# Three weight buffers of 48 KB filled by 6 MB transfers, and 128 rows of one expert's weights on the lower 64 partitions, in a mixture-of-experts layer on one core

## The chip, the cores and the metric

The kernel runs on one core of a Trainium2 chip. The metric is device time in microseconds, the median of three runs. The kernel before takes 968.97 us (968.91 to 969.14). About 0.2% of that, 1.9 us, is what a measurement of this kernel can tell from no change.

On the core, TensorE (PE) multiplies matrices and transposes, VectorE (DVE) and ScalarE (ACT) work on elements and copy results out of PSUM, and SyncE (SP) issues the transfers (DMAs) from the chip's memory (HBM) into the on-chip memory (SBUF). Sixteen DMA engines carry them out.

## The reference

One layer over 272 tokens (16 learned meta tokens and a sequence of 256) of width 1024, all float32:

```
h = layer_norm(alpha * h + pool_mixer(h))      # causal pooling over windows 2, 4, 8, 16
h = layer_norm(alpha * h + moe(h))             # output drops the 16 meta tokens
moe: logits = h @ router_w + router_b; 4 of 32 experts per token, softmax over the 4
     each expert e:  (clamped_swiglu(x @ w1[e] + b1[e]) @ w2[e] + b2[e]) * gate
```

`w1[e]` is 1024 x 2048 (8 MB) and `w2[e]` 1024 x 1024 (4 MB). All 32 experts are used, so 384 MB of weights are read once.

## The kernel before, in words

A prologue (L151 to L338) mixes, normalises and routes the tokens. Each expert has 64 places (`CAP`) for tokens; a branch for more tokens than that stands at the end of the program and is not taken here.

Then a loop over the 32 experts, two to a pair. Of each expert:

- `load_w1` (L345) fetches `w1[e]` as two transfers of 4 MB into two buffers of a ring, each holding four blocks of 128 rows (32 KB on each of 128 partitions). `load_w2` (L355) fetches `w2` as one transfer of 4 MB into a third buffer. The ring has four buffers (`W_BUFS`). A load is issued on SP's queue when the buffer it takes has been read for the last time; SP issues in the order of the program.
- `mlp_in` (L388) is 8 steps over the blocks k of `w1`, four matmuls each: the expert's 64 gathered tokens are the stationary operand and the weights stream past. Steps 0 to 3 need the first transfer, 4 to 7 the second.
- `swiglu` (L399): ACT copies the two halves out of PSUM (`hs`, L403), PE transposes them back (L406), DVE and ACT apply bias, clamp and gate.
- `finish(e - 1)` runs `mlp_out` (L436) of the expert before: 16 matmuls with `w2[e - 1]` as the streaming operand, and two copies into `y`.
- For an odd expert, `combine` (L458) adds the pair before to `acc` by matmuls with `srow` (L462), and `prepare` (L539) gathers the next pair's tokens (`gather`, L131, matmuls at L138).

From expert 28 on the sums are kept in PSUM: `onto` (L561, L566) takes the place of `combine`. Expert 29 is finished in its own iteration (L613 to L617), so its `w2` is loaded right after its `w1`. The last transfers are `w1[31]` (8 MB, in pieces), `w2[30]` (4 MB) and `w2[31]` in two column halves (`load_w2_halves`, 4 MB, in pieces); behind them `mlp_out_half` (L447, L451) does expert 31 by halves, then come the last sums, the layer norm (`store`, L492) and four output transfers.

The order on each engine is the program's, except where `tc.issue_after` moves a block behind a named instruction. In the printed order a matmul on float32 counts once, in the profile twice.

Of the kernel before, what the change touches and what calls it, by code (L numbers as in the profile page):

```python
# [17 lines left out]
P = 128  # L18
# [15 lines left out]
W_BUFS = 4  # L34
# [7 lines left out]
def moe_trunk(ctx: ExitStack, tc: tile.TileContext, x, pool_w, aux_in, b1_in, w1, w2, w2_last, b2, out):  # L42
# [46 lines left out]
    b2r = const.tile([E + 1, D], F32, name="b2r")  # L89
# [62 lines left out]
    b1_b = const.tile([P, D], F32, name="b1_b")  # L152
    xg0 = columns()
    d0 = mid.tile([P, NT, 2, CAP], F32, tag="disp", name="d0")
    with tc.tile_pool(name="pro", bufs=1) as pro:
# [5 lines left out]
        pw = pro.tile([P, G, 2, GD], F32, name="pw")  # L161
# [45 lines left out]
        uT = pro.tile([P, G, 2, SEQ], F32, name="uT")  # L207
# [137 lines left out]
    def load_w1(src, pieces=((0, 4), (0, 4))):  # L345
        v = src.rearrange("(i p j) f -> i p j f", p=P, j=4)
        ts = []
        for i, js in enumerate(pieces):
            wt = wpool.tile([P, 4, 2 * D], F32, tag="w", name="w1t")
            for j, j2 in zip(js, js[1:]):  # L350
                nc.sync.dma_start(out=wt[:, j:j2], in_=v[i][:, j:j2])
            ts.append(wt)
        return lambda k: ts[k // 4][:, k % 4, :]

    def load_w2(src, js=(0, KC)):  # L355
        v = src.rearrange("(p j) f -> p j f", j=KC)
        wt = wpool.tile([P, KC, D], F32, tag="w", name="w2t")
        for j, j2 in zip(js, js[1:]):
            nc.sync.dma_start(out=wt[:, j:j2], in_=v[:, j:j2])
        return lambda k: wt[:, k, :].rearrange("p (c o s) -> p o c s", c=2, o=2)  # L360

    def load_w2_halves():

        ts = wpool.tile([P, 2, KC, 512], F32, tag="w", name="w2h")
# [23 lines left out]
    def mlp_in(xcols, w1k):  # L388
        ph = [bank_h() for _ in range(2)]
        for k in range(KC):  # L390
            wk = w1k(k)
            for u in range(2):
                for hf in range(2):
                    last[k // 4] = nc.tensor.matmul(ph[u][hf * CAP:(hf + 1) * CAP], lhsT=xcols(k),  # L394
                                                    rhs=wk[:, u * D + hf * 512:u * D + (hf + 1) * 512],
                                                    start=(k == 0), stop=(k == KC - 1))
        return ph

    def swiglu(ph, bias, banks=(bank_t, bank_t)):  # L399
        pre = []  # L400
        for u in range(2):
            hs = work.tile([P, 512], F32, tag="hs", name="hs", bufs=3)
            nc.scalar.copy(hs, ph[u])  # L403
            pt = banks[u]()
            for j in range(4):
                nc.tensor.transpose(pt[:, j * P:(j + 1) * P], hs[:, j * P:(j + 1) * P], ident)  # L406
            a = work.tile([P, KC, CAP], F32, tag=f"a{u}", name=f"a{u}", bufs=1)
            nc.vector.tensor_add(a, pt.rearrange("p (c s) -> p c s", s=CAP),  # L408
                                 bias[:, :, u].unsqueeze(2).to_broadcast([P, KC, CAP]))
# [45 lines left out]
    def outputs():  # L455
        return work.tile([P, 2, 512], F32, tag="y", name="y", bufs=2)
# [13 lines left out]
    def add_rest():  # L470

        for i in range(2):
            sl = slice(i * 512, (i + 1) * 512)
            p = spread(g0T, i, bank_o())
            for t in range(NT):
                r = work.tile([P, 512], F32, tag="hs", name="rest", bufs=3)
                nc.vector.tensor_mul(r, h[:, t, sl], p)
                nc.vector.scalar_tensor_tensor(acc[:, t, sl], r, DN_ALPHA, acc[:, t, sl], op0=ALU.mult, op1=ALU.add)
# [3 lines left out]
        gT = work.tile([E + 1, SEQ], F32, name="gT")  # L482
# [29 lines left out]
    def overflow():  # L512

        with tc.For_i(0, E, 1) as e:
# [8 lines left out]
            w1k = load_w1(w1[ds(e, 1)].rearrange("e d f -> (e d) f"))  # L523
            w2k = load_w2(w2[ds(e, 1)].rearrange("e d f -> (e d) f"))
# [12 lines left out]
    pairs, acts, w2s, last = {}, {}, {}, [None, None]  # L537

    def prepare(pair, to=bank_t, banks=(bank_o, bank_o)):  # L539
        d = dispatched(place[:, :, 2 * pair:2 * pair + 2])  # L540
        s = slot_rows(d, gates[:, :, 2 * pair:2 * pair + 2], to)
        xg = columns()
        gather(d, xg, banks)
        pairs[pair] = s, outputs(), xg

    def finish(e, to=bank_y):
        pair, i = divmod(e, 2)
        mlp_out(acts[e], w2s[e], pairs[pair][1], i, to)

    pairs[0] = None, None, xg0  # L550
# [19 lines left out]
    for e in range(E):  # L570
        pair, i = divmod(e, 2)
        w1k = load_w1(w1[e], ((0, 4), (0, 4)) if e < E - 1 else ((0, 2, 4), (0, 2, 3, 4)))

        for x in range(max(e - 1, 0), e + (e == E - 3)):
            if e <= E - 3:
                w2s[x] = load_w2(w2[x])
        if i == 0:
            xg = pairs[pair][-1]
        ph = mlp_in(lambda k: xg[k // 4][:, k % 4, i * CAP:(i + 1) * CAP], w1k)
        if e == 0:  # L580
            with tc.issue_after(last[1].ins):
                pairs[0] = slot_rows(d0, gates[:, :, 0:2]), outputs(), xg0
        elif e < E - 3 and i and pair:
            s, y, _ = pairs[pair - 1]
            with tc.issue_after(last[0].ins):
                combine(y, s, pair == 1)
        elif e == E - 3:
            s, y, _ = pairs[pair - 1]
            with tc.issue_after(last[0].ins):
                onto(y, s, slice(0, 512))  # L590
# [112 lines left out]
```

## Time and profile before

| | |
|---|---|
| median of three runs | 968.97 us |
| the profiled execution, own time | 969.74 us |
| its span, first to last instruction | 968.0 us |
| PE busy | 890.0 us (92% of the span) |
| DVE, ACT busy | 237.9, 133.0 us |
| mean granted TensorE clock | 0.976 of full speed |
| moved from and to HBM | 407 MB, 420 GB/s over the span |

The span leaves 1.74 us of the execution's own time outside it. A row of the timeline or of the chain of waits gives the start in us from the start of the span, the duration, the engine, the line of the kernel and what is written and read (`ps_h<-w1t,xg`: the PSUM tile `ps_h` from `w1t` and `xg`). In square brackets stands how long the engine was idle before and who ended that. A window's row gives the busy time of each engine in a stretch, then the granted TensorE clock (PEclk), the mean busy share of the 16 DMA engines and the GB/s that they moved. L394 is `mlp_in`, L443 `mlp_out`, L451 `mlp_out_half`, L406 the transposes of `swiglu`, L462 and L566 the sums over a pair, L138 the gather.

### The profile page before, as it was taken

What the parts mean: (1) busy time and instruction counts of PE and PEld (TensorE: products, weight loads), DVE (VectorE), ACT (ScalarE), POOL (GpSimd) and SP (SyncE); (2) the same over time, 40 slices, a digit from 0 to 9 for tenths busy, and PEclk for the clock granted to TensorE, in tenths of its full rate; (3) what the DMA queues carried; (4) which work ended last, traced back from release to release, by engine and by line L of the source; (5) the groups of instructions that cost most, each with busy time, mean ns of one, the idle gap of its engine ahead of it and who ended that gap; (6) DMA issues with size and microseconds to landing.
All of it is one profiled execution on the core that took longest, in us unless ns stands there. A gap on an engine that the chain in (4) does not pass through costs nothing.

```text
span 968.0 us, 9685 instructions
## 1 busy us (share of the span) xinstructions
PE 890.0 (92%) x4229; PEld 374.4 (39%) x4229; DVE 237.9 (25%) x495; ACT 133.0 (14%) x271; POOL 1.1 (0%) x9
## 2 busy tenths in 40 slices
PE   9999899979899899998989989899898989999994
PEld 7443433424334343343433334343343433334332
DVE  7331122212152131121311223122121311212024
ACT  1320100201002010020201102010020100102011
POOL 0000000000000000000000000000000000000000
PEclk9999999999999999999999999999899999999998
DMA  9999999999999999999999999999999999999992
GB/s 384 429 427 430 431 430 431 431 433 428 431 429 430 429 433 430 432 431 430 430 431 429 430 433 431 429 431 429 430 430 431 432 432 433 433 429 426 423 416 108
DMA packets 16937, 407.09 MB, mean 421 GB/s; under 512 B 1883, under 2 KB 2011, under 8 KB 3580
## 3 DMA queue, kind: packets, MB, share of 16 engines
q1 hardware_dynamic: 16848, 406.30, 98.0%
q8 instruction: 35, 0.57, 0.2%
q10 hardware_dynamic: 44, 0.14, 0.0%
q14 instruction: 10, 0.08, 0.0%
HBM read 405.38 MB, written 1.05 MB: 420 GB/s over the span
## 4 chain that ended last, share of the span: by engine, by line
PE 53%; DMA 45%; DVE 1%; issue 0%; ACT 0%; SPq 0%; DVEq 0%; ACTq 0%
DMA w1t<-in_w 40%; PE ps_h L394 24%; PE ps_y L443 11%; PE ps_o L138 5%; PE ps_o L462 5%; DMA w2t<-in_w 3%; DMA w2h<-in_w_last 2%; PE ps_t L406 2%; PE ps_t L180 1%; PE ps_t L443 1%; PE ps_o L566 0%; PE ps_y L103 0%; PE ps_o L489 0%; PE ps_h L227 0%; PE ps_h L138 0%; PE ps_y L451 0%
## 5 line engine op out<-in xcount | busy, mean ns | idle before, releaser
L394 PE MATMUL ps_h<-w1t,xg 128*64 128x512 f32 x2048 | 471.3, 614 | 46.6 <-DMA w1t<-in_w 46.6
L394 PEld LDWEIGHTS ps_h<-w1t,xg 128*64 128x64 f32 x2048 | 157.6, 141 | 343.6 <-issue 334.4
L443 PE MATMUL ps_y<-w2t,act 128*64 128x512 f32 x928 | 205.5, 595 | 10.2 <-DMA w2t<-in_w 9.4
L408 DVE TENSOR_TENSOR a<-ps_t,b 128x512 f32<-128x512 f32 x60 | 41.5, 692 | 401.7 <-PE ps_t L406 398.6
L443 PEld LDWEIGHTS ps_y<-w2t,act 128*64 128x64 f32 x928 | 67.5, 137 | 128.7 <-issue 113.6
L403 ACT COPY hs<-ps_h 128x512 f32<-128x512 f32 x64 | 37.5, 586 | 350.6 <-PE ps_h L394 350.4
L468 DVE TENSOR_TENSOR acc<-acc,ps_o 128x512 f32<-128x512 f32 x48 | 33.0, 688 | 137.0 <-PE ps_o L462 137.0
L138 PE MATMUL ps_o<-disp,h 128*128 128x128 f32 x448 | 59.1, 275 | 0.0
L138 PEld LDWEIGHTS ps_o<-disp,h 128*128 128x128 f32 x448 | 55.4, 192 | 7.0 <-issue 7.0
L434 DVE COPY y<-ps_y 64x512 f32<-64x512 f32 (+1 forms) x30 | 20.4, 680 | 121.8 <-PE ps_y L443 120.9
L462 PE MATMUL ps_o<-y,srow 128*128 128x512 f32 x104 | 48.1, 605 | 0.0
L143 ACT ACTIVATE xg<-ps_o,aux 128x128 f32<-128x128 f32 x56 | 21.2, 456 | 178.1 <-PE ps_o L138 178.1
L432 ACT COPY y<-ps_y 64x512 f32<-64x512 f32 x29 | 16.8, 580 | 202.6 <-DVE y L434 202.6
L406 PE MATMUL ps_t<-ident,hs 128*128 128x128 f32 x240 | 39.3, 286 | 1.9 <-ACT hs L403 0.3
L406 PEld LDWEIGHTS ps_t<-ident,hs 128*128 128x128 f32 x240 | 25.2, 141 | 32.0 <-ACT hs L403 30.1
L462 PEld LDWEIGHTS ps_o<-y,srow 128*128 128x128 f32 x104 | 18.7, 189 | 29.2 <-issue 29.2
L416 DVE TENSOR_TENSOR a<-a,sig 128x512 f32<-128x512 f32 x32 | 22.1, 692 | 10.7 <-ACT sig L414 10.7
L414 ACT ACTIVATE sig<-a 128x512 f32<-128x512 f32 x32 | 20.1, 630 | 29.8 <-DVE a L412 27.3
L146 DVE TENSOR_SCALAR xg<-ps_o,aux 128x128 f32<-128x128 f32 x60 | 22.8, 405 | 2.8 <-PE ps_o L138 2.7
L418 DVE SCALAR_TENSOR_TENSOR act<-a,a 128x512 f32<-128x512 f32 x32 | 22.0, 687 | 0.6
L415 DVE TENSOR_SCALAR a<-a 128x512 f32<-128x512 f32 x32 | 13.5, 421 | 0.0
L412 DVE TENSOR_SCALAR a<-a 128x512 f32<-128x512 f32 x32 | 13.4, 418 | 0.1
(165 smaller groups left out, 260.0 us busy)
## 6 DMA issues: line engine op xcount, KB each, us to landing
w1t<-in_w SPq DMA_DIRECT2D x62, 4096.0 KB, 30.0
w2t<-in_w SPq DMA_DIRECT2D x30, 4096.0 KB, 29.3
w1t<-in_w SPq DMA_DIRECT2D x3, 2048.0 KB, 27.2
w2t<-in_w SPq DMA_DIRECT2D x4, 1024.0 KB, 25.4
w2h<-in_w_last SPq DMA_DIRECT2D x3, 1024.0 KB, 21.0
w1t<-in_w SPq DMA_DIRECT2D x2, 1024.0 KB, 30.4
xT<-in_x SPq DMA_DIRECT2D x2, 544.0 KB, 5.7
pw<-in_pool_w SPq DMA_DIRECT2D x2, 512.0 KB, 7.0
```

The lines of the kernel that those rows point to most:

```text
L138: nc.tensor.matmul(p[:, (k % n) * P:(k % n + 1) * P], lhsT=h[:, t, k * P:(k + 1) * P], rhs=d[:, t].rearrange("p i s -> p (i s)"), start=(t ...
L143: gx = nc.scalar.activation(xg[0][:, k, :], pk, AF.Identity, scale=g0T[:, k:k + 1], bias=b0T[:, k:k + 1])
L146: nc.vector.tensor_scalar(xg[1][:, k - 4, :], pk, g0T[:, k:k + 1], b0T[:, k:k + 1], op0=ALU.mult, op1=ALU.add)
L394: last[k // 4] = nc.tensor.matmul(ph[u][hf * CAP:(hf + 1) * CAP], lhsT=xcols(k), rhs=wk[:, u * D + hf * 512:u * D + (hf + 1) * 512], start ...
L403: nc.scalar.copy(hs, ph[u])
L406: nc.tensor.transpose(pt[:, j * P:(j + 1) * P], hs[:, j * P:(j + 1) * P], ident)
L408: nc.vector.tensor_add(a, pt.rearrange("p (c s) -> p c s", s=CAP), bias[:, :, u].unsqueeze(2).to_broadcast([P, KC, CAP]))
L416: nc.vector.tensor_mul(gate, gate, sig)
L418: nc.vector.scalar_tensor_tensor(act.rearrange("p c s -> p (c s)"), up.rearrange("p c s -> p (c s)"), 1.0, gate.rearrange("p c s -> p (c s ...
L443: nc.tensor.matmul(py[o], lhsT=act[:, 2 * j + hf, :], rhs=wk[:, o], start=(n == 0), stop=(n == KC - 1))
L462: nc.tensor.matmul(p, lhsT=s[:, o, t * P:(t + 1) * P], rhs=y[:, o, :], start=True, stop=True)
L468: nc.vector.tensor_add(a, a, pv)
```

## The change

- The ring has three buffers of 48 KB on each partition in place of four of 32 KB (144 KB for 128 KB).
- The weights lie in HBM in two tensors with rows of 48 KB. `wp[e]` holds `w2[e - 2]` and blocks 0 and 1 of `w1[e]`; `wq[e]` holds blocks 2 to 7 of `w1[e]`. From expert 2 on an expert is two transfers of 6 MB, `wp[e]` and `wq[e]`.
- `finish(e - 2)` runs ahead of `mlp_in(e)`, where `finish(e - 1)` ran behind it. Expert 29 is finished in iteration 31, and the sum of its pair moves there too.
- Expert 0 takes `wq[0]` first and its blocks in the order 2 to 7, 0, 1. Blocks 0 and 1 of experts 0 and 1 share a buffer. Block 1 of expert 1 (128 rows, 1 MB) lies as two halves of 64 rows side by side on partitions 0 to 63, and comes in eight transfers of eight partitions each (r, r + 8, ... r + 56, 16 KB on each); its step of `mlp_in` is two steps with 64 rows each.
- To make room: `pw` and `uT` of the prologue lie in the ring's first buffer (`early`), `b2r` in `b1_b`, `gT` in an `hs` buffer, `sig` in `act`, the last `y` in `acc`; `hs` has two buffers for three and `y` one for two.

```diff
-W_BUFS = 4
+W_BUFS = 3
...
+    def ring(name):
+        return wpool.tile([P, 6 * 2 * D], F32, tag="w", name=name)
...
+        early = ring("early")
+        pw = early[:, :G * 2 * GD].rearrange("p (g c d) -> p g c d", g=G, c=2)
...
+    def w1_of(t, t2, at=W2):
+        def w1k(k):
+            f = at + 2 * D * k if k < 2 else 2 * D * (k - 2)
+            return (t if k < 2 else t2)[:, f:f + 2 * D]
+        return w1k
...
+    def load_q(src, ks=(0, 6)):
+        return load(ring("wq"), src, [2 * D * k for k in ks])
...
+        t, t2 = load(ring("w2t"), wp[E], [D * k for k in (0, 2, 4, 6, 8)]), ring("w2h")
+        ts = [v.rearrange("p (k d) -> p k d", d=512) for v in (t[:, W2:], t2[:, :KC * 512])]
...
-            hs = work.tile([P, 512], F32, tag="hs", name="hs", bufs=3)
+            hs = work.tile([P, 512], F32, tag="hs", name="hs", bufs=2)
...
-        return work.tile([P, 2, 512], F32, tag="y", name="y", bufs=2)
+        return work.tile([P, 2, 512], F32, tag="y", name="y", bufs=1)
...
-        w1k = load_w1(w1[e], ((0, 4), (0, 4)) if e < E - 1 else ((0, 2, 4), (0, 2, 3, 4)))
-
-        for x in range(max(e - 1, 0), e + (e == E - 3)):
-            if e <= E - 3:
-                w2s[x] = load_w2(w2[x])
+        if e < 2:
+            wt2 = load_q(wq[e])
+            if e == 0:
+
+
+                wt = ring("wp")
+                nc.sync.dma_start(out=wt[:, :4 * D], in_=wp[0, :, W2:])
+                nc.sync.dma_start(out=wt[:, 4 * D:6 * D], in_=wp[1, :, W2:W2 + 2 * D])
+                for r in range(8):
+                    nc.sync.dma_start(out=wt[r:CAP:8, 6 * D:10 * D], in_=w1_low[r:CAP:8])
+            w1k = w1_of(wt, wt2, 4 * D * e)
+        else:
+
+            wt = load(ring("wp"), wp[e], (0, 6 * 2 * D))
+            w1k = w1_of(wt, load_q(wq[e], (0, 6) if e < E - 1 else (0, 2, 4, 5, 6)))
+            finish(e - 2, w2_of(wt))
...
+            xl = small.tile([CAP, CAP], F32, name="xl", bufs=1)
+            nc.scalar.copy(xl, xg[0][CAP:, 1, CAP:])
+            low = [(x, wt[:CAP, f:f + 2 * D]) for x, f in ((xg[0][:CAP, 1, CAP:], 6 * D), (xl, 8 * D))]
+        ph = mlp_in(lambda k: xg[k // 4][:, k % 4, i * CAP:(i + 1) * CAP], w1k,
+                    range(KC) if e else (2, 3, 4, 5, 6, 7, 0, 1), low)
...
-        if 0 < e < E - 4:
-            finish(e - 1)
...
-        if E - 4 <= e < E - 2:
-            finish(e - 1)
...
-            finish(e, t0)
-            s, y, _ = pairs[pair]
-            onto(y, s, slice(0, 512))
```

PE in the middle of the loop, a pair's first expert and the start of its second. Before: `mlp_in` (`w1t`) of one expert, its transposes, `mlp_out` (`w2t`) of the expert before, the next `mlp_in` with the sum of the last pair (L462) in its middle:

```order
L394 MATMUL ps_h<-w1t,xg_3224 64x512 x16
L394 MATMUL ps_h<-w1t,xg_3225 64x512 x16
L406 MATMUL ps_t_3314<-ident,hs 128x128 x4
L406 MATMUL ps_t_3323<-ident,hs 128x128 x4
L443 MATMUL ps_y<-w2t,act 64x512 x16
L394 MATMUL ps_h<-w1t,xg_3224 64x512 x16
L462 MATMUL ps_o_3377<-y,srow 128x512
```

After: `mlp_out` (L453, now from `wp`) ahead of each `mlp_in` (L405: 8 from `wp`, 24 from `wq`), and the sum (L472) behind it:

```order
L453 MATMUL ps_y<-wp,act 64x512 x16
L405 MATMUL ps_h<-wp,xg_3139 64x512 x8
L405 MATMUL ps_h<-wq,xg_3139 64x512 x8
L405 MATMUL ps_h<-wq,xg_3140 64x512 x16
L417 MATMUL ps_t_3227<-ident,hs 128x128 x4
L417 MATMUL ps_t_3236<-ident,hs 128x128 x4
L453 MATMUL ps_y<-wp,act 64x512 x16
L405 MATMUL ps_h<-wp,xg_3139 64x512 x8
L405 MATMUL ps_h<-wq,xg_3139 64x512 x8
L405 MATMUL ps_h<-wq,xg_3140 64x512 x16
L472 MATMUL ps_o_3306<-y,srow 128x512
```

`mlp_out` has moved from behind an expert's transposes to ahead of its `mlp_in`, and waits with it for the same transfer.

PE at the end. Before, from `mlp_out` of expert 29 (`ps_t_3697`) and the sum of its pair (L566) on, then experts 30 and 31:

```order
L443 MATMUL ps_t_3697<-w2t,act 64x512 x16
L566 MATMUL ps_o_3514<-y,srow 128x512
L394 MATMUL ps_h<-w1t,xg_3668 64x512 x16
L394 MATMUL ps_h<-w1t,xg_3669 64x512 x16
L406 MATMUL ps_t_3760<-ident,hs 128x128 x4
L394 MATMUL ps_h<-w1t,xg_3668 64x512
L406 MATMUL ps_y<-ident,hs 128x128 x4
L394 MATMUL ps_h<-w1t,xg_3668 64x512 x15
L394 MATMUL ps_h<-w1t,xg_3669 64x512 x16
L406 MATMUL ps_t_3826<-ident,hs 128x128 x4
L443 MATMUL ps_h<-w2t,act 64x512 x16
L451 MATMUL ps_h<-w2h,act 64x256 x8
```

After, from the end of `mlp_in` of expert 30 on: its transposes, `mlp_out` of expert 29, `mlp_in` of expert 31, the sum of pair 14 (L580), then as before:

```order
L405 MATMUL ps_h<-wq,xg_3570 64x512 x16
L417 MATMUL ps_t_3657<-ident,hs 128x128 x4
L417 MATMUL ps_y<-ident,hs 128x128 x4
L453 MATMUL ps_y<-wp,act 64x512 x16
L405 MATMUL ps_h<-wp,xg_3569 64x512 x8
L405 MATMUL ps_h<-wq,xg_3569 64x512 x8
L405 MATMUL ps_h<-wq,xg_3570 64x512 x16
L580 MATMUL ps_o_3440<-y,srow 128x512
L417 MATMUL ps_t_3745<-ident,hs 128x128 x4
L453 MATMUL ps_h<-w2t,act 64x512 x16
L461 MATMUL ps_h<-w2t,act 64x256 x8
```

`mlp_out` of expert 29 and its pair's sum (the first of its four rows is shown in both) stood ahead of `mlp_in` of expert 30 and now stand on either side of `mlp_in` of expert 31.

SP's last loads. Before:

```order
L351 DMA w1t<-in_w 128x8192 x2
L351 DMA w1t<-in_w 128x4096 x3
L351 DMA w1t<-in_w 128x2048 x2
L359 DMA w2t<-in_w 128x2048 x4
L367 DMA w2h<-in_w_last 128x2048 x3
L367 DMA w2h<-in_w_last 128x1024
L367 DMA w2h<-in_w_last 128x512 x2
```

After:

```order
L366 DMA wp<-in_wp 128x12288
L366 DMA wq<-in_wq 128x4096 x2
L366 DMA wq<-in_wq 128x2048 x2
L366 DMA w2t<-in_wp 128x2048 x4
L378 DMA w2t<-in_w_last 128x2048 x2
L378 DMA w2h<-in_w_last 128x2048
L378 DMA w2h<-in_w_last 128x1024
L378 DMA w2h<-in_w_last 128x512 x2
```

Behind the last full transfer stood 16 MB in pieces (`w1[31]`, `w2[30]`, `w2[31]`); behind `wp[31]` stand 14 MB.

## Rows read from the trace of the kernel before

**Rows 1.** The page's parts on DMA queues (packets, MB, share of 16 engines), on the chain that ended last, and its first row on DMA issues (count, KB each, median us from issue to landing).

```profile
q1 hardware_dynamic: 16848, 406.30, 98.0%
q8 instruction: 35, 0.57, 0.2%
...
PE 53%; DMA 45%; DVE 1%; issue 0%; ACT 0%; SPq 0%; DVEq 0%; ACTq 0%
...
w1t<-in_w SPq DMA_DIRECT2D x62, 4096.0 KB, 30.0
```

**Rows 2.** Windows of 58.35 us (a pair of experts) in the loop: the stretch, PE, PEld, DVE, ACT and POOL busy, PEclk, DMA share, GB/s.

```profile
129.48:187.83 58.35, 53.64 (x252) 21.87 (x250) 12.93 (x26) 7.37 (x15) 0.00 (x0) 0.97 1.00 430
304.53:362.88 58.35, 54.31 (x256) 22.24 (x254) 13.28 (x27) 7.38 (x15) 0.00 (x0) 0.97 1.00 430
537.93:596.28 58.35, 53.72 (x252) 22.32 (x250) 12.95 (x26) 7.37 (x15) 0.00 (x0) 0.97 1.00 431
```

**Rows 3.** The same view at the end: while the 1 MB pieces land (rows of 8 KB on each partition), and the last 12 us of the transfers.

```profile
926.00:941.00 15.00, 14.86 (x72) 5.32 (x68) 3.43 (x6) 3.38 (x5) 0.00 (x0) 1.00 1.01 420
941.00:944.00 3.00, 2.33 (x10) 0.48 (x8) 0.45 (x1) 0.00 (x0) 0.00 (x0) 1.00 0.98 399
944.00:947.00 3.00, 2.84 (x20) 1.75 (x22) 0.24 (x1) 0.58 (x1) 0.00 (x0) 1.00 0.65 266
947.00:950.00 3.00, 2.91 (x22) 1.25 (x18) 0.05 (x1) 0.00 (x0) 0.00 (x0) 1.00 0.48 180
950.00:953.00 3.00, 2.82 (x24) 1.95 (x24) 0.58 (x2) 0.37 (x1) 0.00 (x0) 1.00 0.09 33
```

**Rows 4.** PE's timeline near the end, from the wait for the second half of `w1[30]` (expert 30, blocks 4 to 7) on.

```profile
911.57 7.09 PE L394 MATMUL ps_h<-w1t,xg 128*64 128x512 f32 x32 [0.78 <-DMA w1t<-in_w]
918.59 0.66 PE L406 MATMUL ps_t<-ident,hs 128*128 128x128 f32 x4
...
941.57 1.94 PE L443 MATMUL ps_h<-w2t,act 128*64 128x512 f32 x8 [0.17 <-DMA w2t<-in_w]
944.16 1.95 PE L451 MATMUL ps_h<-w2h,act 128*64 128x256 f32 x16 [0.66 <-DMA w2h<-in_w_last]
...
950.18 0.40 PE L451 MATMUL ps_y<-w2h,act 128*64 128x256 f32 x1 [0.28 <-DMA w2h<-in_w_last]
```

**Rows 5.** The chain of waits at the end (start, us, what): the last transfer in it, the last matmul on a weight, what follows it.

```profile
929.08 20.97 DMA w2h<-in_w_last
...
955.07 0.06 PE ps_t L451
955.12 0.02 issue
955.14 0.38 ACT y L432
```

**Rows 6.** The chain of waits in the loop: `mlp_out`, the sum of a pair, half an `mlp_in`, a group of transposes.

```profile
535.56 7.04 PE ps_y L443 x32
...
569.49 8.78 PE ps_h L394 x32
578.27 3.63 PE ps_o L462 x8
...
584.14 7.02 PE ps_h L394 x32
591.15 0.59 PE ps_t L406 x4
```

**Rows 7.** PE's longest waits in the loop (us in total, times, longest).

```profile
PE ps_h L394 <- DMA w1t<-in_w: 46.6, 25, 3.1
PEld ps_t L406 <- ACT hs L403: 30.1, 44, 0.8
```

**Rows 8.** SP's timeline at the start: the first four loads, then the first that waited for a buffer; and PE's first `mlp_in` and the last matmul of the prologue's mixing.

```profile
3.78 3.34 SPq L351 DMA_DIRECT2D w1t<-in_w  x4
39.26 0.33 SPq L359 DMA_DIRECT2D w2t<-in_w  x1
47.14 11.73 SPq L351 DMA_DIRECT2D w1t<-in_w  x2
...
16.26 1.89 PE L227 MATMUL ps_o<-uT,pw 128*128 128x256 f32 x8
32.13 7.09 PE L394 MATMUL ps_h<-w1t,xg 128*64 128x512 f32 x32
```

More of the change, by code (lines that the diff above doesn't have):

```diff
@@ L342, in moe_trunk, with w2_of, load, load_last @@
     acc = work.tile([P, NT, D], F32, name="acc")
[L345 to L364, printed above, removed]
+    W2 = KC * D
+    def w2_of(t):
+        v = t[:, :W2].rearrange("p (n c o s) -> p n o c s", n=KC, c=2, o=2)
+        return lambda k: v[:, k]
+    def w1_of(t, t2, at=W2):
[3 more added lines that the diff above has]
+        return w1k
+    def load(t, src, cuts):
+        for f, f2 in zip(cuts, cuts[1:]):
+            nc.sync.dma_start(out=t[:, f:f2], in_=src[:, f:f2])
+        return t
+    def load_q(src, ks=(0, 6)):
+        return load(ring("wq"), src, [2 * D * k for k in ks])
+    def load_last():
+        t, t2 = load(ring("w2t"), wp[E], [D * k for k in (0, 2, 4, 6, 8)]), ring("w2h")
+        ts = [v.rearrange("p (k d) -> p k d", d=512) for v in (t[:, W2:], t2[:, :KC * 512])]
         for c, pieces in enumerate(((0, 4, 8), (0, 4, 6, 7, 8))):
             for k, k2 in zip(pieces, pieces[1:]):
-                nc.sync.dma_start(out=ts[:, c, k:k2], in_=w2_last[c, :, k:k2])
-        return [ts[:, c] for c in range(2)]
+                nc.sync.dma_start(out=ts[c][:, k:k2], in_=w2_last[c, :, k:k2])
+        return w2_of(t), ts
     def dispatched(places):
@@ L386, in slot_rows, with mlp_in @@
         return s
-    def mlp_in(xcols, w1k):
+    def mlp_in(xcols, w1k, ks=range(KC), low=None):
         ph = [bank_h() for _ in range(2)]
[L390 to L396, printed above, removed]
+        for n, k in enumerate(ks):
+            for x, wk in low if low and k == 1 else [(xcols(k), w1k(k))]:
+                for u in range(2):
+                    for hf in range(2):
+                        last[n // 4] = nc.tensor.matmul(ph[u][hf * CAP:(hf + 1) * CAP], lhsT=x,
+                                                        rhs=wk[:, u * D + hf * 512:u * D + (hf + 1) * 512],
+                                                        start=(n == 0), stop=(n == KC - 1))
         return ph
@@ L543, in prepare, with finish @@
         gather(d, xg, banks)
-        pairs[pair] = s, outputs(), xg
-    def finish(e, to=bank_y):
+        pairs[pair] = s, xg
+    def finish(e, w2k, to=bank_y):
         pair, i = divmod(e, 2)
-        mlp_out(acts[e], w2s[e], pairs[pair][1], i, to)
-    pairs[0] = None, None, xg0
+        if i == 0:
+            ys[pair] = outputs()
+        mlp_out(acts[e], w2k, ys[pair], i, to)
+    pairs[0] = None, xg0
     z = []
@@ L571, in moe_trunk @@
         pair, i = divmod(e, 2)
[L572 to L579 removed]
+        if e < 2:
+            wt2 = load_q(wq[e])
+            if e == 0:
+                wt = ring("wp")
+                nc.sync.dma_start(out=wt[:, :4 * D], in_=wp[0, :, W2:])
[7 more added lines that the diff above has]
+            finish(e - 2, w2_of(wt))
+        if i == 0:
+            xg = pairs[pair][1]
+        low = None
+        if e == 1:
+            xl = small.tile([CAP, CAP], F32, name="xl", bufs=1)
[3 more added lines that the diff above has]
+                    range(KC) if e else (2, 3, 4, 5, 6, 7, 0, 1), low)
         if e == 0:
             with tc.issue_after(last[1].ins):
[L582 to L584 removed]
+                pairs[0] = slot_rows(d0, gates[:, :, 0:2]), xg0
+        elif i and pair:
+            s = pairs[pair - 1][0]
             with tc.issue_after(last[0].ins):
[L586 to L589, printed above, removed]
[L590 removed]
+                if e < E - 3:
+                    combine(ys[pair - 1], s, pair == 1)
+                else:
+                    onto(ys[pair - 1], s, slice(0, 512))
         if e == E - 4:
```

46 lines of the change are left out of this document (25 added, 21 removed).

## The prediction

> **What bounds the kernel now.** I read the shares of the DMA queues first. The one queue that carries the data keeps the 16 engines busy for 98.0% of the span, and the chain that ended last is 45% DMA [rows 1]. In the windows of a pair the DMA share is 1.00 and the rate 430 GB/s, pair after pair, while PE works 53.6 to 54.3 of 58.35 us [rows 2]. So in the loop the transfers set the pace, and PE has 4 to 4.7 us of room per pair. PE's waits say the same: 46.6 us in all for `w1t`, never over 3.1 at once [rows 7]. That the loads keep up without a hole is read from their 30.0 us from issue to landing [rows 1]: a 4 MB transfer moves in 9.75 us (4.19 MB at 430 GB/s), so some two others lie queued ahead of each.
>
> The end is another stage. From 911.57, where PE gets the second half of `w1[30]`, to its last matmul on a weight at 955.13, PE waits for a transfer only 0.17, 0.66 and 0.28 us [rows 4, 5]. What counts there is both when the last large load lands and how much PE has left to do from then on. After 955.13 come 12.87 us (to 968.0) that the change does not touch.
>
> **The change part by part.**
>
> *Buffers, in the loop: nothing.* The bytes stay the same. With three buffers of 6 MB, `wq[e + 1]` takes the buffer of `wp[e]`. That is free when PE has done `mlp_out` (7.04) and two of the eight steps (a quarter of 2 x 7.02, 3.5) [rows 6], 10.6 us after `wp[e]` landed. SP reaches the load then. The engines need it when `wp[e + 1]` is done, two transfers of 14.6 us (6.29 MB at 430) after the landing, at 29.2. PE is late by up to some 6 us in an odd expert (`mlp_in` 10.5 behind `wq`, sum 3.63, transposes and gather 5, against 14.6), so 12 us of cover are left. If a buffer came late, SP's later loads would queue behind it and every microsecond would be lost. PE's own sum per pair stays that of [rows 2], inside 58.35. `mlp_out` no longer covers the copy to `hs` in every place; that wait is 0.8 us at a time (30.1 in 44) [rows 7], inside the 4 us of room. The waits for 6 MB instead of 4 MB can be longer (some 4 us), and behind one wait of 2.64 us half an `mlp_in` took 8.78 instead of 7.02 us [rows 6]; two of those per pair still fit into the room.
>
> *Start: nothing.* Before, four loads of 4 MB could go out ahead of PE's first `mlp_in` at 32.13, and the fifth waited until 39.26 [rows 8]. Now it is 6, 2, 1, 1 and 6 MB, 16 MB again. `wq[1]` waits for `early`, free when the mixing ends at about 18.2 [rows 8]; the 10 MB ahead of it last until 34. `wp[2]` waits for `wq[0]`, six steps behind 32.1, at 42.7; the 16 MB last until about 48. The half-row step of expert 1 costs PE four more matmuls, 1.8 us, once, in front of a wait for a load. `xl`, the shared tiles and the smaller rings (`hs`, `y`, `sig`) add no work to PE; their copies lie beside it.
>
> *Rows of 48 KB: -2.4 us.* The engines move 430 GB/s with rows of 32 KB [rows 2] and 420 with rows of 8 KB [rows 3]. Per engine that is 1219 ns for 32 KB as one row and 1248 as four, so 9.7 ns for each row more. Per 96 KB the change has two rows for three. 62 transfers of 6 MB are 24.4 MB per engine, 248 times 96 KB: 2.4 us less at the end of the loop. Rows of 48 KB do not occur before. The bounds: windows in the loop scatter by 1 GB/s, slices of the page by some 0.5% with no cause shown, so 2.4 -/+ 2.7 us. I take 2.4, the value that the two nearest row lengths give.
>
> *The eight-partition transfers: -1.2 us.* The engines do not end together: the share falls from 0.98 over 0.65 and 0.48 to 0.09 within 9 us [rows 3]. Summed from 941 (3 us times 0.98, 0.65, 0.48, 0.09), the mean engine is done at 947.6, the last about 952. If eight partitions go to eight engines, the 1 MB takes 2.4 us more on those and 2.4 less on the others (1.05 MB is 2.44 us on sixteen engines). Where the late engines are among the others, the last one can gain 2.4; where they are among the eight, it loses 2.4. No row says which. Instruction loads are 35 of 16 KB [rows 1] and are the only uneven load that I see. I take half of the gain, since an engine of the early half, now 2.4 us later, can become the last.
>
> [...]
>
> *The end: PE has more left.* Behind the second half of `w1[30]` 16 MB were still to come; behind `wp[31]` it is 14 MB. With the same bytes in all, `wp[31]` is there 2 MB later than 911.57: plus 4.9 (2.10 MB at 430), 916.45. With -2.4 and -1.2 it is 912.85. `mlp_out` of expert 29 needs it whole. PE is free just before: `wq[30]` is there 14.6 us earlier, three quarters of `mlp_in` take 10.5, the transposes some 2.3. From there PE does in a row:
>
> - `mlp_out` of 29: 7.04; `mlp_in` of 31: 14.04; the sum of pair 14: 3.63; two groups of transposes: 1.3 [rows 6];
> - `mlp_out` of 30: 7.0; then what stood between 944.16 and 955.13 less its wait of 0.28 and small gaps: 10.6 [rows 4, 5].
>
> That is 43.6 us, 10.7 of which (`mlp_out` of 29 and the pair's sum) PE used to do before 903. The transfers need only 34.0 us for the 14 MB, so from here PE sets the end: 912.85 + 43.6 = 956.45.
>
> *The sum.* 956.45 against 955.13 is +1.3 us: a span of 969.3, an execution of 971.05 (1.74 outside the span), against 969.74 of the profiled one. The median of the runs is 0.77 below that one, so I predict 970.3 us, +0.14%. A change under 0.2% can't be told from none. With the two unseen terms at their ends (rows -5.1 to +0.3, engines -2.4 to 0) `wp[31]` is there between 909 and 916.8 and the median lies between 966.4 and 974.2; the likely part of that is 968 to 972.5.
>
> **The rivals.**
>
> *The end follows the transfers, not PE (faster).* For it: the last stretch of the chain is 20.97 us of `w2h` [rows 5]. If PE makes up the 10.7 us, or if the sum above counts what overlaps, the kernel ends 3.6 us (2.4 + 1.2) earlier: 965.4. Against it: PE's sum is of rows that stand one after the other, and 43.6 is 9.6 more than 34.0.
>
> *The eight-partition transfers hit the wrong engines, or are slow (slower).* The 128 KB on each of eight engines must go somewhere. If the late engines are among the eight, `wp[31]` is there at 916.45 - 2.4 + 2.4, and the median is 973.9. It decides as soon as the eight engines lose more than about 5 us against the others, half the spread seen in [rows 3]. The same is reached if the transfers run at half speed (4.9 us more on those eight): about 974.5.
>
> [...]
>
> *Neither term exists.* Long rows gain nothing and the late engines stay late: `wp[31]` at 916.45, 973.9 us.
>
> *The queue runs dry in the loop.* If a buffer is late by 1 us once a pair, 15 us are lost: 985. Against it stand the 12 us of cover.
>
> **How the numbers follow.** The forecast has 0.50 (0.04 of it faster, 0.33 same, 0.13 slower), the end that follows the transfers 0.18, the wrong or slow engines 0.20 (0.03 same), neither term 0.07, a dry queue 0.05. That makes faster 0.22, same 0.36, slower 0.42. The range 966.2 to 975.0 holds the forecast, the wrong engines and most of the faster case's neighbourhood, and leaves out the dry queue and the lower half of the faster case.
>
> **What would show it.** Right: a DMA share of 1.00 in the windows of the loop, at 431 to 432 GB/s; PE waiting about 4 us for `wq` in odd experts; the wait for `wp[31]` ending near 913; no wait on a transfer from there on; the last weight matmul near 956.5; DMA share ending in a steeper fall. Wrong: PE waiting for `w2h` pieces at the end (the first rival); the fall of the share as long as before or longer, with `wp[31]` after 916 (the second and third); windows with a share under 0.98 in the loop (the dry queue).

## The result and the profile after

The changed kernel takes 979.61 us (median of six runs, 977.92 to 981.43) against 969.12 for the kernel before: ratio 1.0108, 95% interval 1.0097 to 1.012. It is 1.1% slower, 9.3 us above the forecast of 970.3 and outside the range of 966.2 to 975.0. The profiled execution took 979.66 us with a span of 977.8.

The page of the changed kernel: GB/s in 40 slices of 24.4 us, and the data queue [rows 1] with its share of the engines.

```profile
GB/s 380 309 443 424 443 423 439 426 435 429 425 441 419 445 422 443 423 439 425 433 431 435 429 431 435 425 440 423 439 427 433 431 435 433 431 431 433 413 382 49
...
q1 hardware_dynamic: 12656, 406.30, 97.1%
```

The second slice stands out: 309 GB/s where the loop has some 431. The windows of that place show when (columns as in [rows 2]):

```profile
26.00:31.00 5.00, 3.98 (x34) 3.35 (x33) 1.99 (x11) 3.49 (x8) 0.00 (x0) 1.00 0.97 406
32.00:37.00 5.00, 5.00 (x30) 2.31 (x30) 2.91 (x12) 0.98 (x5) 0.00 (x0) 1.00 0.57 123
```

From 32 to 37 us the engines are busy for 0.57 of the time but move only 123 GB/s. SP's timeline says what is on the queue then: `wq[0]`, two pieces of `wp` (L592, L593), the eight transfers of eight partitions (L595), and the next 6 MB, `wq[1]`, only at 36.51. Behind it stand the last three of the eight by themselves, and in a fence of their own SP's waits there (us in total, times, longest).

```profile
3.80 0.73 SPq L366 DMA_DIRECT2D wq<-in_wq  x1
4.57 0.56 SPq L592 DMA_DIRECT2D wp<-in_wp  x1
5.17 0.59 SPq L593 DMA_DIRECT2D wp<-in_wp  x1
5.80 30.58 SPq L595 DMA_DIRECT2D wp<-in_w_low  x8
36.51 0.36 SPq L366 DMA_DIRECT2D wq<-in_wq  x1
...
26.40 0.56 SPq L595 DMA_DIRECT2D wp<-in_w_low  x1
31.32 0.56 SPq L595 DMA_DIRECT2D wp<-in_w_low  x1
35.82 0.56 SPq L595 DMA_DIRECT2D wp<-in_w_low  x1
```

```profile
SPq L595 <- DMA wq<-in_wq: 15.3, 1, 15.3
SPq L595 <- DMA wp<-in_wp: 8.3, 2, 4.3
```

The sixth of the eight waits for `wq[0]` (15.3 us), the seventh and eighth for the two pieces of `wp` (8.3 us in two): each of the three waits for the load eight places before it on the queue. `wq[1]` stands behind them all, though its buffer is free from 18 us on (the third run below issues it at 18.02), and when it is issued, the eight engines that have no part in these transfers have had nothing to do for some 5 us (16 packets are under way at 31 us, 9 at 33 and 8 from 35.5 to 37.5).

The single packets of the trace, which its views don't list, add the rest: the 64 packets of 16 KB that the eight transfers consist of take a median of 1.273 us, where the 128 packets of the same size just before (L592) take 0.611. Summed up over the data queue, with a packet under way counted by its share, they give the MB moved by a time:

```
MB moved by            30 us   40 us   50 us   60 us   900 us
kernel before          11.29   15.59   19.87   24.18   385.21
changed kernel         11.35   13.20   16.94   21.27   383.37
```

2.93 MB are missing at 50 us, 6.8 us at 432 GB/s. In the loop the changed kernel is faster: from 60 to 900 us it makes good 1.07 MB, 2.5 us. The same window of both, kernel before first:

```profile
100.00:900.00 800.00, 742.28 (x3478) 305.49 (x3474) 181.05 (x347) 102.20 (x209) 0.00 (x0) 0.98 1.00 430
```

```profile
100.00:900.00 800.00, 737.63 (x3471) 301.88 (x3472) 182.90 (x353) 101.72 (x211) 0.00 (x0) 0.97 1.00 432
```

The end, where [rows 4] and [rows 5] stood for the kernel before: PE gets `wp[31]` at 920.80 and works from there to its last matmul on a weight, which starts at 964.93 and ends at 964.99, without a wait for a transfer (PE's timeline, and one row of the chain of waits).

```profile
920.80 8.69 PE L453 MATMUL ps_y<-wp,act 128*64 128x512 f32 x32 [2.65 <-DMA wp<-in_wp]
929.31 3.61 PE L405 MATMUL ps_h<-wp,xg 128*64 128x512 f32 x16
932.75 10.48 PE L405 MATMUL ps_h<-wq,xg 128*64 128x512 f32 x48
943.16 2.84 PE L580 MATMUL ps_o<-y,srow 128*128 128x512 f32 x6
945.84 1.02 PE L580 MATMUL ps_t<-y,srow 128*128 128x512 f32 x2
947.66 7.09 PE L453 MATMUL ps_h<-w2t,act 128*64 128x512 f32 x32
954.58 1.90 PE L461 MATMUL ps_h<-w2t,act 128*64 128x256 f32 x16
```

```profile
964.93 0.06 PE ps_t L461
```

From there to the end of the span are 12.8 us, as before (12.87).

### The profile page after: what moved, and what is told of

It reads as the page before. It is cut to its first block, busy times and chain, and to the rows that moved or that the text cites. A ratio compares the mean times of both kernels' runs of the same rounds, so it can differ in the third digit from the quotient of the medians.

```text
span 977.8 us, 9661 instructions
## 1 busy us (share of the span) xinstructions
PE 890.8 (91%) x4237; PEld 371.9 (38%) x4237; DVE 236.7 (24%) x495; ACT 132.1 (14%) x272; POOL 1.1 (0%) x9
## 4 chain that ended last, share of the span: by engine, by line
PE 55%; DMA 43%; DVE 2%; issue 0%; ACT 0%; DVEq 0%
DMA wq<-in_wq 37%; PE ps_h L405 26%; PE ps_y L453 12%; DMA wp<-in_wp 6%; PE ps_o L144 5%; PE ps_o L472 5%; PE ps_t L417 1%; PE ps_t L186 1%; PE ps_h L453 1%; PE ps_o L580 1%; PE ps_o L499 1%; PE ps_h L461 0%; PE ps_t L393 0%; PE ps_h L233 0%; PE ps_y L461 0%; DVE xg L518 0%
## 5 line engine op out<-in xcount | busy, mean ns | idle before, releaser
L405 PE MATMUL ps_h<-wq,xg 128*64 128x512 f32 x1536 | 356.9, 623 | 51.3 <-DMA wq<-in_wq 51.3
L453 PE MATMUL ps_y<-wp,act 128*64 128x512 f32 x960 | 218.1, 607 | 16.4 <-DMA wp<-in_wp 12.3
L405 PEld LDWEIGHTS ps_h<-wq,xg 128*64 128x64 f32 x1536 | 114.7, 144 | 290.1 <-issue 224.9
L453 PEld LDWEIGHTS ps_y<-wp,act 128*64 128x64 f32 x960 | 71.7, 139 | 142.4 <-issue 121.2
L405 PE MATMUL ps_h<-wp,xg 128*64 128x512 f32 (+1 forms) x512 | 116.9, 593 | 0.0
L419 DVE TENSOR_TENSOR a<-ps_t,b 128x512 f32<-128x512 f32 x60 | 40.2, 688 | 266.3 <-PE ps_t L417 264.7
L405 PEld LDWEIGHTS ps_h<-wp,xg 128*64 128x64 f32 (+1 forms) x512 | 38.9, 137 | 70.3 <-issue 70.2
L444 DVE COPY y<-ps_y 64x512 f32<-64x512 f32 x30 | 20.7, 689 | 157.3 <-PE ps_y L453 157.3
L144 PE MATMUL ps_o<-disp,h 128*128 128x128 f32 x448 | 54.7, 275 | 0.0
L472 PE MATMUL ps_o<-y,srow 128*128 128x512 f32 x104 | 48.1, 605 | 0.0
L472 PEld LDWEIGHTS ps_o<-y,srow 128*128 128x128 f32 x104 | 18.7, 189 | 29.2 <-issue 29.2
L427 DVE TENSOR_TENSOR a<-a,act 128x512 f32<-128x512 f32 x32 | 22.1, 692 | 16.9 <-ACT act L425 16.9
L425 ACT ACTIVATE act<-a 128x512 f32<-128x512 f32 x32 | 20.2, 632 | 30.7 <-DVE a L423 30.3
```

The lines of the kernel that those rows point to most:

```text
L144: nc.tensor.matmul(p[:, (k % n) * P:(k % n + 1) * P], lhsT=h[:, t, k * P:(k + 1) * P], rhs=d[:, t].rearrange("p i s -> p (i s)"), start=(t ...
L405: last[n // 4] = nc.tensor.matmul(ph[u][hf * CAP:(hf + 1) * CAP], lhsT=x, rhs=wk[:, u * D + hf * 512:u * D + (hf + 1) * 512], start=(n == ...
L427: nc.vector.tensor_mul(gate, gate, act)
L444: nc.vector.tensor_copy(y[r, o, cols], py[o])
L453: nc.tensor.matmul(py[o], lhsT=act[:, 2 * j + hf, :], rhs=wk[:, o], start=(n == 0), stop=(n == KC - 1))
L472: nc.tensor.matmul(p, lhsT=s[:, o, t * P:(t + 1) * P], rhs=y[:, o, :], start=True, stop=True)
```

## The experiments

The theory after the result: the eight transfers cost the 6.8 us, by two mechanisms, a slow destination (packets of 1.27 us) and the held-back queue (`wq[1]` at 36.5). Rivals: their source in HBM is slow; or the order of the three buffers, not the eight transfers, starves the start. The other open question is the end, where PE sets the time.

**Where the rows land, or where they come from.** The first run changes only the partitions of the eight transfers, the second only their addresses in HBM (the rows lie in HBM in another order).

```diff
-                for r in range(8):
-                    nc.sync.dma_start(out=wt[r:CAP:8, 6 * D:10 * D], in_=w1_low[r:CAP:8])
+                for r in range(8):                                    # first run
+                    a = r % 4 + 32 * (r // 4)
+                    nc.sync.dma_start(out=wt[a:a + 29:4, 6 * D:10 * D], in_=w1_low[r:CAP:8])
...
+                    nc.sync.dma_start(out=wt[r:CAP:8, 6 * D:10 * D], in_=w1_low[8 * r:8 * r + 8])   # second run
```

> The eight transfers of w1_low write partitions four apart (r, r + 4, ... r + 28, then the same from 32 on) instead of eight apart; their addresses in HBM are as before (rows eight apart). In the changed kernel 115 to 131 GB/s are moved while they run (32 to 37 us). Theory A, the destination: eight partitions eight apart share ways into SBUF in pairs; four apart they don't, so the stretch moves about 215 GB/s (half of 430) and is 5 us shorter: about 974 to 976 us. Theory B, the source: rows 128 KB apart in HBM are slow; nothing changes, 979 to 980 us and 115 to 131 GB/s. Theory C, only the held-back queue counts (SP issues the next 6 MB at 36.5 since it waits for the transfers eight before): the rate may change, but the time stays above 978.

> The eight transfers write the same partitions as in the changed kernel (eight apart), but each reads eight rows that lie one behind the other in HBM (128 KB in one piece) instead of rows 128 KB apart. Theory A (destination): no change, 115 to 131 GB/s in the stretch and 979 to 980 us. Theory B (source): about 215 GB/s there and 974 to 976 us.

Measured: 973.5 us (ratio to the kernel before 1.0047, 1.003 to 1.0063; half a us better than expected) with partitions four apart, 979.13 (1.0101, 1.0084 to 1.0118) with other addresses. The window from 33 to 35 us, in which little but the eight transfers runs (of the pieces of L593, three packets of 8 KB in the changed kernel and one in the second run): changed kernel, first run, second run.

```profile
33.00:35.00 2.00, 2.00 (x11) 0.77 (x12) 1.90 (x8) 0.00 (x0) 0.00 (x0) 1.00 0.63 127
```

```profile
33.00:35.00 2.00, 2.00 (x14) 0.58 (x10) 1.82 (x7) 0.00 (x0) 0.00 (x0) 1.00 0.53 221
```

```profile
33.00:35.00 2.00, 2.00 (x13) 0.89 (x13) 1.53 (x8) 0.36 (x3) 0.00 (x0) 1.00 0.59 119
```

At a similar busy share of the engines the rate goes from 127 to 221 GB/s with the partitions, and stays at 119 with the addresses. The packets of 16 KB take 0.611 us in the first run and 1.276 in the second. The destination it is; the source has no part in it. In the first run the eighth transfer also waits less long, so `wq[1]` goes out at 34.36 instead of 36.51: a part of its gain is the queue's.

**The plain transfer (third run).** The eight transfers and the two half-row steps go; block 1 of expert 1 comes like its neighbour.

```diff
-                for r in range(8):
-                    nc.sync.dma_start(out=wt[r:CAP:8, 6 * D:10 * D], in_=w1_low[r:CAP:8])
+                nc.sync.dma_start(out=wt[:, 6 * D:8 * D], in_=wp[1, :, W2 + 2 * D:W2 + 4 * D])
```

> Block 1 of expert 1 comes as one transfer of 128 partitions with rows of 8 KB, as its neighbour block does; the eight transfers and the half-row matmuls are gone, the buffers of 48 KB stay. Theory: the 2.9 MB (6.8 us) by which the changed kernel is behind at 50 us come from the eight transfers alone, so the next 6 MB are issued near 18 us, the engines never run short there, and the time is 979.6 - 6.8 = 972.8 us, still above the kernel before (969.1), because the tail then stands at +4.9 - 2.4 and PE's work behind it. Rival: the deficit comes from the order of the three buffers at the start; then 978 to 980 us.

Measured: 972.75 us (1.0036, 1.0024 to 1.0049). `wq[1]` is issued at 18.02, 19.83 MB are moved at 50 us (19.87 before), 386.24 at 900 (385.21 before). So all of the start's loss comes with the eight transfers, and none from the three buffers.

```profile
18.02 0.33 SPq L366 DMA_DIRECT2D wq<-in_wq  x1
```

What is left, 3.8 us over the kernel before, is the end.

**The held-back queue (sixth and seventh run).** In both kernels `wq[1]` is issued behind the fifth of the eight transfers instead of the eighth, once with partitions four apart, once eight apart.

```diff
-                for r in range(8):
+                for r in range(5):
...
+            else:                      # e == 1, behind load_q(wq[1])
+                for r in range(5, 8):
```

> As the first run (partitions four apart, 973.5 us), but the next 6 MB (wq[1]) are issued behind the fifth of the eight transfers instead of behind the eighth, so SP waits only for wq[0] and not for the two pieces behind it. Theory (the held-back queue costs what the first run is behind the plain load): wq[1] is issued near 26.5, the 2 us by which the first run lands wp[31] later than the third go, 971.5 to 973 us; if the late engines were among the other eight, another 2 us less (970). Rival: the eight that get 128 KB more hold late engines too, so the last engine is 1 to 1.5 us later than in the third run: 973.5 to 974.5 us.

> The changed kernel with its partitions eight apart, and only the order of the sixth run: wq[1] issued behind the fifth of the eight transfers. Theory A alone (the slow destination is all of the loss): no change, 979 to 980 us. Held-back queue: the engines that have nothing to do from 31.5 to 37.6 us work on wq[1] in that time, 2 to 4 us less, 975.5 to 978 us; the packets of the eight still take twice as long.

Measured: 973.2 us (1.0046, 1.0029 to 1.0063) and 979.81 (1.0112, 1.0095 to 1.0129). With partitions four apart the queue is indeed held back no longer: `wq[1]` goes out at 26.23, and 24.09 MB are moved at 60 us against 23.26 in the first run, 1.9 us. But `wp[31]` lands no earlier: PE has it at 915.70, against 915.87 in the first run and 913.91 with the plain transfer, and the time, between what I had expected and the rival, can't be told from the first run's. The rows of the plain transfer, the first and the sixth run, and SP's of the sixth:

```profile
913.91 8.78 PE L453 MATMUL ps_y<-wp,act 128*64 128x512 f32 x32 [2.63 <-DMA wp<-in_wp]
```

```profile
915.87 8.53 PE L453 MATMUL ps_y<-wp,act 128*64 128x512 f32 x32 [2.64 <-DMA wp<-in_wp]
```

```profile
915.70 7.09 PE L453 MATMUL ps_y<-wp,act 128*64 128x512 f32 x32 [2.29 <-DMA wp<-in_wp]
...
26.23 0.34 SPq L366 DMA_DIRECT2D wq<-in_wq  x1
```

With partitions eight apart nothing is won, a miss of the expectation: 18.46 MB at 50 us are 1.5 more than in the changed kernel, but the last three transfers, now behind 6 MB, land so late (their last packet ends at 59.6 us) that PE stands idle for 6.7 us before its half-row step of expert 1, which starts at 60.94; the buffer comes free late, and `wq[2]` is issued at 68.06 instead of 57.26; at 60 us 21.49 MB are moved against 21.27.

Why the 1.9 us don't arrive is read from the packets, chained engine by engine (each starts as the one before it on its engine ends, in the changed kernel within 0.02 us). "The eight" are the engines that carry the eight transfers. Ends of one 6 MB transfer early in the loop, and of one late in it, on the sixteen engines, us:

```
                          early on: others / the eight     near 870 or 900: others / the eight
plain transfer            48.1 to 50.7 (all)                891.5 to 898.7 (all)
first run                 50.5 to 52.5 (all)                893.8 to 900.7 (all)
wq[1] behind the fifth    60.9 to 62.3 / 65.2 to 66.9       up to 868.1 / 864.9 to 871.4
changed kernel            54.5 to 54.8 / 56.0 to 57.3       897.9 to 904.4 / 899.7 to 905.6
```

In these chains eight engines lose some 1.5 us at a time, three or four times each between 60 and 905 us, 29 times in all in the changed kernel. In that stretch the queue of the instruction loads has 29 packets of 16 KB (35 in the whole run [rows 1]); each takes some 1.06 us and stands in a gap of that length, and the packet of 48 KB behind it takes 2.3 us instead of 1.82. Of these engines, six are among the others and two among the eight that carry the extra 128 KB. A transfer has landed when its last engine is done (in the changed kernel the last three engines end `wp[31]` at 918.90, 919.63 and 920.14, and PE has it at 920.80), and the last ones are those two. So the extra rows relieve six late engines and push two further back; the spread near 900 us is 7.7 us in the changed kernel and 7.2 with the plain transfer.

**What makes a destination slow.** In the changed kernel each of the eight transfers (r, r + 8, ... r + 56) holds four pairs of partitions 32 apart, and its packets took 1.273 us; in the first run a transfer (r, r + 4, ... r + 28) holds none, and they took 0.611. Three runs of one execution each (the tenth to twelfth) test whether it is these pairs: in the first two no transfer holds one, in the third each transfer is one.

```diff
+                    nc.sync.dma_start(out=wt[8 * r:8 * r + 8, ...     # eight behind one another
...
+                for r in range(16):                                   # sixteen of four, eight apart
+                    a = r % 8 + 32 * (r // 8)
+                    nc.sync.dma_start(out=wt[a:a + 25:8, ...
...
+                for r in range(32):                                   # thirty-two of two, 32 apart
+                    nc.sync.dma_start(out=wt[r:CAP:32, ...
```

> The changed kernel, but each of the eight transfers writes eight partitions one behind the other (8 r to 8 r + 7). [...] If any eight partitions that aren't four apart cost the same: 979 to 980 us and 115 to 131 GB/s.

> The same 64 rows, now in sixteen transfers of four partitions, eight apart (r, r + 8, r + 16, r + 24, then the same from 32 on), so that no two partitions of a transfer are 32 apart; four engines do the work. If partitions 32 apart share a way into SBUF (which halves eight rows eight apart): packets of 16 KB take 0.61 us. If rows eight apart are slow as such: 1.2 to 1.3 us. The kernel is slower than the changed one either way, since four engines carry 256 KB each: 980 to 990 us.

> The same 64 rows in thirty-two transfers of two partitions, 32 apart (r and r + 32); two engines do the work. If partitions 32 apart share a way: packets of 16 KB take 1.2 us though only two engines run. If not: 0.61 us. The kernel is far slower either way, since two engines carry 512 KB each (20 us at 0.61, 39 us at 1.2): about 990 to 1000 us in the one case, 1005 to 1020 in the other.

Measured: 980.48, 978.17 and 998.73 us. The first two miss what was expected and lie in the range of the changed kernel's six executions (977.92 to 981.43), the third misses the range for slow pairs; so what decides are the packets. The 64 packets of 16 KB in order of length, us:

```
                              shortest   quarter   median   three quarters   longest
eight apart (changed kernel)     0.652     1.132    1.273            1.287     1.307
four apart                       0.611     0.611    0.611            0.619     0.727
eight behind one another         0.745     1.164    1.176            1.302     1.716
four, eight apart                0.608     0.611    0.612            0.619     1.241
two, 32 apart                    0.614     0.908    1.238            1.286     2.045
```

Four partitions eight apart take 0.612 us, as four apart do, so eight apart is not slow as such. Two partitions 32 apart take 1.238 us, twice as long, with only two engines at work (a busy share of 0.13 of sixteen from 33 to 59 us): the two of such a pair slow each other, and the changed kernel's transfers consist of four such pairs. Not all of the packets in the last row are slow, and the time, 998.73, lies in the range that I had given for none being slow (990 to 1000). In order of time the short ones, of 0.6 to 1.1 us, come in eight runs of two to five, one about every eight packets, that is every four transfers; why, no run shows. Two things don't fit pairs alone. Eight partitions behind one another hold no such pair in a transfer and are slow all the same: the median is 1.176 us, the longest of the first packets 1.7, and the stretch from 32 to 37 us moves 93 GB/s, less than the 115 to 131 that I had given for a cost like the changed kernel's. And the first packets of `wq[1]`, 48 KB each, take 3.46 to 3.89 us instead of 1.82 beside the eight transfers; in the first run the first of them took up to 2.57. Both stay open.

**The end.** PE is the last to finish; so pieces that let it start earlier should help. First the changed kernel with `wp[31]` split, then the plain transfer with more pieces.

```diff
-            wt = load(ring("wp"), wp[e], (0, 6 * 2 * D))
+            wt = load(ring("wp"), wp[e], (0, 6 * 2 * D) if e < E - 1 else (0, W2, 6 * 2 * D))       # fourth run
...
+            wt = load(ring("wp"), wp[e], (0, 6 * 2 * D) if e < E - 4 else (0, W2, 6 * 2 * D))       # fifth run
+            ... load_q(wq[e], (0, 6) if e < E - 5 else (0, 3, 6) if e < E - 1 else (0, 2, 4, 5, 6))
...
+            ... (0, W2, 12 * D) if e < E - 1 else (0, 4 * D, W2, 12 * D)                            # ninth run
```

> The last wp transfer (6 MB) is issued as two: the 4 MB of w2[29] first, then the 2 MB of w1[31]. The rest is the changed kernel. Theory (PE sets the end): PE starts the second matrix of expert 29 when it has nothing else to do, at 918.2 instead of 920.8, and without the wait of 2.65 us before it the 1.7 us at half clock go too: 4.3 us less, 975.3 us. Rival (the end follows the transfers): nothing moves, 979 to 980 us.

> As the third run (block 1 of expert 1 as one plain transfer), and from expert 27 on each 6 MB load comes in two pieces: wq[27] to wq[30] as 3 + 3 MB, wp[28] to wp[31] as the 4 MB of w2 and the 2 MB of w1. Theory (PE sets the end, because it waits for whole 6 MB transfers beforehand): the waits of 2.6 to 5 us for wq[27], wq[29] and wp[31] in the third run shrink by what a piece lands earlier, so PE is ahead by 3 to 7 us at the end: 966 to 970 us, and no wait of PE over 1 us behind 880. Rival (PE's waits before 880 are not what delays the end, the transfers are): 972 to 973 us.

> As the fifth run, but wp[31] comes as three pieces of 2 MB, two of them w2[29]. In the fifth run PE waits 3.05 us for the 4 MB of w2[29] and then does its 32 matmuls in 10.05 instead of 7.09 us, much of it at half clock. Theory: the first half of w2[29] lands 4.9 us earlier, before PE asks or shortly after; the wait falls under 1 us, the half clock behind it goes too, and PE is 4 to 5 us earlier at its last weight (956.3 in the fifth run), where the last transfer (949.1) begins to count: 965.5 to 967.5 us. Rival (the sum over a pair and the next pieces are late next): no more than 1 us, 968.5 to 970 us.

Measured: 977.56 us (1.0087, 1.0071 to 1.0104), 969.75 (1.0003, 0.9994 to 1.0013) and 967.05 (0.9981, 0.9972 to 0.999). The 32 matmuls of expert 29 in the fourth, fifth and ninth run:

```profile
919.15 7.09 PE L453 MATMUL ps_y<-wp,act 128*64 128x512 f32 x32 [0.78 <-DVE a L419]
```

```profile
909.90 10.05 PE L453 MATMUL ps_y<-wp,act 128*64 128x512 f32 x32 [3.05 <-DMA wp<-in_wp]
```

```profile
907.31 7.09 PE L453 MATMUL ps_y<-wp,act 128*64 128x512 f32 x32 [0.78 <-DVE a L419]
914.36 3.65 PE L405 MATMUL ps_h<-wp,xg 128*64 128x512 f32 x16
919.27 3.65 PE L405 MATMUL ps_h<-wq,xg 128*64 128x512 f32 x16 [1.26 <-DMA wq<-in_wq]
```

In the fourth run PE starts 1.65 us earlier and is 1.60 faster, 3.25 in all and not the 4.3 expected, since it now waits 0.78 us for DVE (L419); 2.0 us arrive. In this build the sum over the pair stands inside `mlp_in`, in two parts: 0.5 us of the 3.25 are gone when both are done (944.10 against 946.86), and 0.5 more by the start of `mlp_out` of expert 30 (945.42 against 947.66), as the sum no longer covers the copies that the transposes wait for. In the fifth run the 4 MB of `w2[29]` are still awaited for 3.05 us (a miss: I had expected no wait over 1 us), and the matmuls behind that wait take 10.05 us. With 2 MB pieces wait and slow stretch are gone, and the last weight is done near 952 where the fifth run has 956.4. This version is faster than both kernels, against the kernel before by 0.1 to 0.3% only, about the least that can be told.

**Row length (eighth run).** The plain transfer, all loads of the loop as two of 3 MB, rows of 24 KB.

```diff
-            wt = load(ring("wp"), wp[e], (0, 6 * 2 * D))
+            wt = load(ring("wp"), wp[e], (0, 6 * D, 6 * 2 * D))
...
+            ... load_q(wq[e], (0, 3, 6) if e < E - 1 else (0, 2, 4, 5, 6))
```

> As the third run (plain load), but every load of 6 MB of the loop comes as two of 3 MB with rows of 24 KB. By 9.7 ns for a row more, 96 KB are four rows in place of two: 248 times 19.4 ns = 4.8 us later at the end of the loop, about 384.2 MB moved at 900 us (third run 386.2, kernel before 385.2). If rows cost nothing: 386.2 MB. The time: the landing of wp[31] as said, less what PE gains by smaller pieces: 970 to 976 us.

Measured: 384.25 MB at 900 us, and 971.78 us (1.0028, 1.0018 to 1.0039). Rows of 48 KB (plain transfer) and of 24 KB, the loop:

```profile
100.00:900.00 800.00, 740.02 (x3476) 303.34 (x3474) 180.13 (x348) 101.37 (x210) 0.00 (x0) 0.97 1.00 432
```

```profile
100.00:900.00 800.00, 732.49 (x3468) 296.15 (x3466) 181.79 (x347) 100.85 (x209) 0.00 (x0) 0.99 1.00 429
```

24, 32 and 48 KB give 429, 430 and 432 GB/s; two rows more per 96 KB cost 1.99 MB, 4.6 us, against 4.8 expected. Here the number of transfers doubles with the rows. That the rows count is told by the packets: the median one takes 0.915 us with 24 KB, 1.216 with 32 (kernel before) and 1.819 with 48, which for 96 KB is 3.660, 3.648 and 3.638 us. Though its transfers are 4.6 us later, this kernel is 1 us faster than the one with 48 KB rows: at the end the smaller pieces are worth more to PE than the rate.

## Why the prediction was wrong

The sum of the forecast, term by term:

- *Start: nothing.* This is the step that failed. I checked when buffers come free and counted 16 MB queued ahead, but not what else a load waits for: eight more loads put `wq[1]` behind transfers that waited for the load eight places before them, the last of them until 35.82 us. And I took the eight transfers at the ordinary rate per engine, where their packets took 1.273 us and not 0.611. Together they cost 6.8 us (2.93 MB at 50 us). Other partitions give back 4.6 us of it (first run, 1.99 MB at 60 us), the order of the queue on top of that 1.9 (sixth run); the order alone, with the slow partitions, gives back 0.5 (seventh run, 0.22 MB at 60 us). So the two do not simply add up.
- *The eight-partition transfers: -1.2.* No run shows this term. That eight partitions go to eight engines was my assumption, and the transfers did run on eight (7.8 of their packets under way on average from 32 to 36 us), but the gain is not there. The late engines lie on both sides, two of them among the eight, and the last of all became later: +1.8 us from the plain transfer to the sixth run (913.91 to 915.70). In the changed kernel the other eight engines stand idle meanwhile, and that lies within the 6.8: `wp[31]` is there 6.9 us later than with the plain transfer (913.91 to 920.80).
- *Rows of 48 KB: -2.4.* Right: 1.03 MB, 2.4 us at 900 us in the plain transfer, and the run with 24 KB rows and its packets bear out the 9.7 ns for a row. (The loop has 61 such transfers and not 62, which is 0.04 us.) In the plain transfer `wp[31]` is there at 913.91; the forecast without its -1.2 is 914.05.
- *Buffers in the loop: nothing.* Right: DMA share 1.00 from 100 to 900 us.
- *The end: PE has more left, 43.6 us.* Right that PE sets the end: 44.2 from 920.80 to 964.99. But 1.65 of it is the slow stretch behind the wait, which I had not counted; without it 42.5 are left, so that the size came out this near is partly luck.

So 912.85 + 6.8 + 1.2 gives 920.85 for `wp[31]` (920.80), and with PE's 44.2 and the 12.8 us behind it the span of 977.8, 8.5 over the forecast's 969.3. The other 0.8 of the 9.3 us lie outside the sum of the stages: I took the median 0.77 below the profiled execution, and here it is 0.05 below; and 1.86 us lie outside the span, for 1.74.

Of the rivals, the one with the slow transfers named the right cause, with half speed, an assumption that the packets bore out (1.273 us for 0.611), and too small a price: it stopped at 974.5, because it let the engines go on with the next load, which SP had not issued yet. The first rival (the end follows the transfers) falls: in the plain transfer the transfers are done at 948 and PE's last weight at 958.13, in the changed kernel at 955 and 964.93.

## What to carry to other kernels

Count a new load's place on its queue, not only its buffer: here a load waited for the one eight before it (15.3 us in one case), so eight small transfers held back the next large one to 36.51 us although its buffer was free at 18. A transfer over few partitions can be slowed by which partitions they are: here packets to rows 32 apart took 1.238 us, to rows four apart within 32 0.611. Look at the length of its packets. Where PE sets the end, first ask what it waits for before: smaller pieces in the last loads (of 2 to 4 MB, then `w2[29]` in two of 2 MB) were worth 5.7 us (972.75 to 967.05), over twice the gain of the longer rows.

## What the runs showed that I had not expected

- The same 16 KB packets at 0.611 and 1.27 us, by nothing but the partitions they are written to.
- PE after a wait. Behind waits of 2.63 to 2.65 us for `w2[29]` (changed kernel, first three runs) its 32 matmuls took 8.53 to 8.79 us, behind 3.05 us 10.05; behind 2.29 and 0.78 they took 7.09. In the changed kernel the granted clock is 0.50 from 922 to 924 us, the lower of the two levels in the trace, 0.50 and 1.00 (PE's busy time, clock, DMA share and GB/s):

```profile
922.00:924.00 2.00, 2.00 (x6) 0.50 0.99 418
```

- The scatter from execution to execution. With 24 KB rows no wait for a load is over 2.0 us, and eight executions of that kernel lie within 0.7 us; the changed kernel's six lie within 3.5. Waits in the loop are not enough to explain it: in the ninth run they reach 4.0 us, and its eleven executions lie within 0.8. The fifth run, with its wait of 3.05 us for `w2[29]`, scatters by 3.7. That the wait near the end is what scatters I did not test.
